# A hybrid attention layer: P's transposed blocks written to DRAM a pair later, and read back behind the next pair's first projection

## The chip, the core and the metric

The kernel runs on one core of a Trainium2 chip. TensorE (PE) multiplies, VectorE (DVE) and ScalarE (ACT) do elementwise work, GpSimd (POOL) and SyncE (SP) here mostly start transfers; transfers are also started from ScalarE's queue. The metric is device time in microseconds (us). The runs of the kernel before are 389.53, 388.30 and 389.66, with a median of 389.53.

## The reference

Input `x` is 512 rows of 1024 numbers, all float32. One layer:

```python
h = rms_norm(x, norm_w)
qa, ka, va, za, qb, kb, vb, zb, gl_a, gl_b = split(h @ w_in)   # eight parts of 512, two of 1024
qa, ka = rms_norm(heads(qa), q_norm_w), rms_norm(heads(ka), k_norm_w)     # 8 heads of 64
oa = moba_attention(qa, ka, va, rel_bias)         # softmax over causal scores plus a bias by distance
ob = stick_breaking_attention(qb, kb, vb)         # weights: sigmoid(z) times a product of (1 - sigmoid)
ya = (merge(oa) * silu(za)) @ w_up_moba
yb = (merge(ob) * silu(zb)) @ w_up_sb
y = sigmoid(gl_a + b_a) * ya + sigmoid(gl_b + b_b) * yb
out = x + y @ w_out
```

With 512 rows in two blocks of 256 and a top 3, the block selection of branch a takes every earlier block, so branch a is a plain causal softmax with a bias. Branch b is strictly causal.

## The kernel before, in words

Every large product is made in float32 accuracy out of three fast matmuls (lines 234 to 236): each operand is split into a high and a low part, ScalarE makes the high part of a weight tile (line 188, `wh<-wr`), VectorE the low part by subtraction (line 190, `wl<-wr,wh`). A weight tile `wr` of 512 KB is loaded by SP (lines 160 and 179). There are three buffers each for `wr`, `wh` and `wl`; a load waits until the low part of the tile three before it is made, and a split waits until TensorE is done with the tile three before.

The middle of the kernel, from 145.6 us on, is a loop over eight pairs of heads (`PAIRS`: pairs 0 to 3 are branch a, pairs 4 to 7 branch b). For a pair:

- TensorE makes the scores of both heads (line 513, `sa` or `sb`), in three groups of two PSUM banks, and then the weighted sum of values of the pair two before (line 608, `po<-pt,v`).
- VectorE and ScalarE turn the scores into weights P. In branch a: bias and row minimum (line 533), exponential (535), scaling (539, 541). In branch b: sigmoids on ScalarE (554, 555, 564, 565), then on VectorE scans (558, 568, `sx<-om`) and products (560, 570, `pb<-pb,sx`).
- P has to be transposed. VectorE transposes 32 by 32 blocks within each quarter of the partitions (line 580, `turned`, two buffers). The quarters are exchanged through DRAM: `put` writes the four quarters with four transfers of 160 KB on SP's queue (line 587, `pda`/`pdb`, four buffers), and `get` reads the whole back with one transfer of 640 KB on ScalarE's queue (line 594, `pta`/`ptb`, four buffers).
- Between these, projections are filled in as TensorE's work: three chunks of 24 matmuls a pair (`FILLS`: `gl` gates, `kb` keys, `zb` gates of branch b, `ya` the up-projection of branch a; pair 7 has more). `finish` multiplies the weighted sum by its gate (line 613, `oa`/`ob`) and splits it (761, 762).

PSUM has two banks named `pj` and six named `s`. A `pj` bank serves a projection or a weighted sum, so the second projection of a pair writes the bank that the weighted sum `po` leaves: it waits for line 613. The six `s` banks serve the scores and `ya`; the products with `ya` are taken out by line 780 (`gl<-ya,gl`).

Each engine executes its own instructions in order, and a queue starts its transfers in order. The order itself is fixed when the program is built, by a scheduler that takes instructions of all engines by data dependence and by its own estimate of when each could start; `tc.issue_after(i)` keeps an instruction behind `i` in that order. Each transfer that SP or ScalarE starts also takes one of eight completion counters in turn, and waits until that counter's last transfer has landed.

At the end of `b` = 1 of pairs 4, 5 and 6, `sum_w` makes sums of output weights by transfers of GpSimd; a copy of one number of `done[m, b]` holds them back until that read-back has landed (line 141).

Of the kernel before, what the change touches and what calls it, by code (L numbers as in the profile page):

```python
# [12 lines left out]
AF = mybir.ActivationFunctionType  # L13
# [28 lines left out]
SUMS = {(4, 1): ("T1a",), (5, 1): ("T1b",), (6, 1): ("T2a",)}  # L42
# [17 lines left out]
def hybrid_layer(ctx: ExitStack, tc: tile.TileContext, x, xT, w, rel, out):  # L60
    nc = tc.nc
    V, A, G, T = nc.vector, nc.scalar, nc.gpsimd, nc.tensor
# [13 lines left out]
    def bank(tag, name):  # L76
        return pp.tile([P, S], F32, tag=tag, bufs=BANKS[tag], name=name)

    def slot(name, dt=F32):
        return gp.tile([P, S], dt, tag="g", name=name)  # L80
# [32 lines left out]
    def wide(name):  # L113

        return vp.tile([P, H // 2, 2, P], F32, tag="v", name=name).rearrange("p a b d -> p (a b d)")
# [23 lines left out]
    def sum_w(names, done):  # L139

        with tc.issue_after(G.tensor_copy(turn_of, done[:1, :1].bitcast(F32)).ins):  # L141
            for n in range(2):
                for name in names:
                    if n == 0:
                        sums[name] = wide(name)
                    blk = TERMS[name[:2]][n]
                    src = sums[blk + name[2]] if blk[0] == "T" else w[WO + BLOCKS.index(blk + name[2])]
                    nc.gpsimd.dma_start(sums[name], src, **({"accum_op": ALU.add} if n else {}))
# [234 lines left out]
    def load_bias(h):  # L383
        bt = oms[h % 2][:, :S]
        nc.sync.dma_start(bt, bass.AP(tensor=e_dr.tensor, offset=e_dr.offset + h * TW, ap=[[1, P], [1, S]]))
        return bt
# [106 lines left out]
    def chunk_ct(name):  # L493
        hi, lo = load_w()
        ps = bank(home[0], name)
        for k in range(KT):
            ks = slice(k * P, (k + 1) * P)
            mm3(ps, hi[:, ks], lo[:, ks], xH[k], xL[k], k == 0, k == KT - 1)
        return ps


    def scores(br, p, q, k, res):

        (qh, ql), (kh, kl) = q[p], k[p]
        for grp in ((3,), (2,), (1, 0)):
            ps = [bank("s", f"s{br}{2 * p + b}{grp[0]}") for b in range(2)]
            c = 0
            for i in grp:
                n = (i + 1) * P
                for m, (x, y) in enumerate(((qh, kl), (ql, kh), (qh, kh))):  # L510
                    for b in range(2):
                        o = slice(b * HD, (b + 1) * HD)
                        T.matmul(ps[b][:, c:c + n], x[o, i * P:(i + 1) * P], y[o, :n], start=m == 0, stop=m == 2)  # L513
                for b in range(2):
                    res[2 * p + b][i] = ps[b][:, c:c + n]
                c += n
            for b in range(2):
                res[2 * p + b][grp] = ps[b][:, :c]
# [25 lines left out]
    evicted = []  # L544
# [31 lines left out]
    def turn(br, h, rows):  # L576
        turned = tp.tile([P, 4, 10, 32], F32, tag="turned", bufs=2, name=f"turned{br}{h}")
        for i, n in ((3, 4), (2, 3), ((1, 0), 3)):
            at = AT[i if i in (3, 2) else 1]
            V.transpose(turned[:, :, at:at + n, :].rearrange("p q j r -> p j q r"),  # L580
                        rows[i].rearrange("p (j q c) -> p j q c", j=n, q=4))
        return turned

    def put(br, h, turned):
        dr = dp.tile([P, 4 * PQ], F32, tag="pd", bufs=4, name=f"pd{br}{h}")
        for a in range(4):
            nc.sync.dma_start(bass.AP(tensor=dr.tensor, offset=dr.offset + a * PQ,
                                      ap=[[4 * PQ, 32], [32 * 4 * PQ, 4], [1, PQ]]),
                              turned[a * 32:(a + 1) * 32].rearrange("c q k r -> c q (k r)"))
        return dr  # L590

    def get(br, h, dr):
        pt = tp.tile([P, 4 * PQ], F32, tag="pt", bufs=4, name=f"pt{br}{h}")
        nc.scalar.dma_start(pt, dr)
        return pt

    ocol = {}
# [17 lines left out]

    zr, qb, kb = {}, [], []

    def f_z(br, p):
        ps = chunk_ct(f"z{br}{p}")
        zr[br, p] = slot(f"z{br}{p}")  # L620
        A.activation(zr[br, p], ps, AF.Sigmoid)
        V.tensor_tensor(zr[br, p], ps, zr[br, p], op=ALU.mult)

    def f_q(p):
# [7 lines left out]
    def f_g(i):  # L632
        ps = chunk_ct(f"gl{i}")
        g = slot(f"gl{i}")
        evicted.append(A.activation(g, ps, AF.Identity if raw[0] else AF.Sigmoid, bias=mb[:, i:i + 1]).ins)  # L635
        gates[i] = g

    raw = [False]

    def f_s(i):  # L640
        with tc.issue_after(evicted[-1]):
# [2 lines left out]
    for i, word in enumerate(FRONT):  # L644
        kind, n = word.split(":")
        f_g(int(n)) if kind == "g" else f_z("a", int(n))
        if i == 0:
            norm(ps_ka, "ka", after=summed[0])
            mix_x(0)
        elif i == 1:  # L650
            mix_x(1)
            summed.append(each(add_sum, "v", ("T3",), last["ka"]))
        elif i == 2:
            bring("qa")
            mix_x(2)
        elif i == 3:
            spread(ps_ka, "ka")
            mix_x(3)
        elif i == 4:
            bring("ka")  # L660
        elif i == 5:
            qa.extend(split_flipped(raws["qa"], "qa"))
# [152 lines left out]
    def split_3(k):  # L815
# [3 lines left out]


    make = {"za": lambda i: f_z("a", i), "zb": lambda i: f_z("b", i), "q": f_q, "k": f_k, "g": f_g, "s": f_s,
            "up": lambda i: up("a", i)}
    fills = [[(kind, int(i)) for kind, i in (word.split(":") for word in part.split())] for part in FILLS]

    def fill(tag="pj"):

        for kind, i in fills.pop(0):
            home[0] = "s" if kind == "up" else tag
            make[kind](i)

    PAIRS = [("a", p) for p in range(H // 2)] + [("b", p) for p in range(H // 2)]
    done = {}

    def head(m, b):
        return PAIRS[m][0], 2 * PAIRS[m][1] + b

    def finish(m, tag="s"):

        br, p = PAIRS[m]
        weighted(tag, br, p, v_of[br], [done.pop((m, b)) for b in range(2)])  # L840
        split_o(br, p)

    early[0] = True
    for m, (br, p) in enumerate(PAIRS):
        raw[0] = br == "a"
        q, k = (qa, ka) if br == "a" else (qb, kb)
        sc = {h: {} for h in (2 * p, 2 * p + 1)}
        with tc.issue_after(end[0]):
            scores(br, p, q, k, sc)
        if m > 1:  # L850
            finish(m - 2, "pj")
        for b in range(2):
            h = 2 * p + b
            bias = load_bias(h) if br == "a" else None
            done[m, b] = put(br, h, turn(br, h, (softmax if br == "a" else stick)(h, sc[h], bias)))
            fill()
            if not b:
                done[m, 0] = get(*head(m, 0), done[m, 0])
        for b in range(2):
            if not b:  # L860
                done[m, 1] = get(*head(m, 1), done[m, 1])
            if (m, b) in SUMS:
                sum_w(SUMS[m, b], done[m, b])
            fill("pj" if (b or not fills[1]) and m < 7 else "s")
    fill()
    for m in (6, 7):
# [160 lines left out]
```

## Time and profile before

| | |
|---|---|
| runs, us | 389.53, 388.30, 389.66 |
| the profiled execution: time, span | 388.29, 386.5 |
| granted TensorE clock | 1.000 |
| TensorE busy | 379.2 us (98%), 1935 matmuls |
| VectorE, ScalarE, GpSimd busy | 284.5, 211.2, 80.0 us |
| loads `wr<-in_w` on SP | 57 of 512 KB, 5.5 us from issue to landing (median) |
| writes `pda`, `pdb` on SP | 32 and 32 of 160 KB, 2.9 and 3.2 us |
| read-backs `pta`, `ptb` on ScalarE's queue | 8 and 8 of 640 KB, 5.1 and 4.9 us |

The time of an execution is 1.8 us more than its span from first to last instruction. Matmuls overlap, so TensorE's busy time is not its floor; the distance between starts of matmuls (0.23 us for 512 columns) shows where it stands still. A row of a timeline has start, duration, engine, line, operation, tiles written and read, partitions and elements, the count, and in square brackets how long the engine had been idle and what ended that. SPq and ACTq are queues that start transfers.

### The profile page before, as it was taken

The numbers are of one execution on the slowest core, as the hardware profiler recorded it, in microseconds if no ns is written. First come the engines' busy times: TensorE is split into PE (matmuls) and PEld (weight loads), VectorE is DVE, ScalarE is ACT, GpSimd is POOL, SyncE is SP. The second block draws the span as 40 slices with busy tenths as digits, with TensorE's granted clock in tenths as the row PEclk, the third lists the DMA queues.
The fourth block names the chain that finished last, engine by engine and source line by source line (L and its number), as shares of the span: only waits on it lengthen the run. The fifth ranks groups of instructions, "written<-read, shape, count | busy, mean of one in ns | idle before, by whom it ended". The sixth has DMA issues, their size and how long they took to land.

```text
span 386.5 us, 5481 instructions
## 1 busy us (share of the span) xinstructions
PE 379.2 (98%) x1935; PEld 308.3 (80%) x1935; DVE 284.5 (74%) x487; ACT 211.2 (55%) x367; POOL 80.0 (21%) x124
## 2 busy tenths in 40 slices
PE   8999999999999999999999999999999999999996
PEld 4888888888888998887878877776777877888885
DVE  4828999945777468972965399599939926999963
ACT  5685567338764447782853494554628213368540
POOL 3859959120210200000000000020101000420310
PEclk9999999999999999999999999999999999999999
DMA  7989799986864745569846826977697784599965
GB/s 264 342 332 336 198 234 274 283 277 238 209 173 100 190 124 187 146 204 335 242 110 207 308 69 213 303 181 226 190 332 257 159 331 132 173 254 294 177 155 175
DMA packets 36747, 86.38 MB, mean 223 GB/s; under 512 B 3944, under 2 KB 16744, under 8 KB 36720
## 3 DMA queue, kind: packets, MB, share of 16 engines
q1 hardware_dynamic: 27696, 52.72, 41.6%
q0 software_dynamic: 6576, 22.57, 24.6%
q10 hardware_dynamic: 2448, 10.75, 8.1%
q8 instruction: 15, 0.25, 0.2%
q14 instruction: 12, 0.10, 0.1%
HBM read 67.65 MB, written 14.70 MB: 213 GB/s over the span
## 4 chain that ended last, share of the span: by engine, by line
PE 82%; DVE 6%; DMA 5%; ACT 3%; issue 2%; SPq 2%; DVEq 0%
PE gl L234 6%; PE gl L235 6%; PE gl L236 6%; DMA pdb<-turnedb 3%; PE sa L513 2%; DMA wr<-in_w 2%; PE yb L234 2%; PE yb L235 2%; PE ka L235 2%; PE ka L234 2%; PE vx L235 2%; PE vx L234 2%; PE za L235 2%; PE za L234 2%; PE ka L236 2%; PE yb L236 2%
## 5 line engine op out<-in xcount | busy, mean ns | idle before, releaser
L190 DVE TENSOR_TENSOR wl<-wr,wh 128x1024 fp32r<-128x1024 f32 (+1 forms) x61 | 71.6, 1178 | 24.5 <-ACT wh L188 24.1
L188 ACT ACTIVATE wh<-wr 128x1024 fp32r<-128x1024 f32 (+1 forms) x61 | 63.2, 1036 | 46.2 <-DMA wr<-in_w 25.1
L234 PE MATMUL gl<-xl,wh 128*128 128x512 f32 x128 | 50.0, 391 | 0.0
L235 PE MATMUL gl<-xh,wl 128*128 128x512 f32 x128 | 49.8, 389 | 0.0
L236 PE MATMUL gl<-xh,wh 128*128 128x512 f32 x128 | 49.8, 389 | 0.0
L141 POOL COPY turn_of<-ptb 1x1 f32<-1x1 f32 x3 | 2.3, 758 | 148.9 <-DMA ptb<-pdb 148.9
L234 PEld LDWEIGHTS gl<-xl,wh 128*128 128x128 f32 x128 | 24.0, 188 | 5.2 <-issue 0.2
L236 PEld LDWEIGHTS gl<-xh,wh 128*128 128x128 f32 x128 | 24.0, 188 | 5.0
L235 PEld LDWEIGHTS gl<-xh,wl 128*128 128x128 f32 x128 | 24.0, 188 | 4.9
L635 ACT ACTIVATE gl<-gl,x 128x512 f32<-128x512 f32 x16 | 11.0, 685 | 20.8 <-PE gl L236 20.0
L533 DVE CUSTOM_DVE_ANT_0 pa<-sa,om 128x512 f32<-128x512 f32 (+3 forms) x32 | 13.9, 483 | 9.5 <-DMA om<-e_dr 6.8
L535 ACT ACTIVATE pa<-pa,m 128x512 f32<-128x512 f32 (+3 forms) x32 | 17.6, 552 | 5.0 <-DVE m L533 5.0
L558 DVE TENSOR_TENSOR_SCAN sx<-om,begin 128x512 f32<-128x512 f32 (+1 forms) x16 | 16.6, 1073 | 0.0
L580 DVE STREAM_TRANSPOSE turneda<-pa 128x384 f32<-128x384 f32 (+1 forms) x24 | 13.8, 605 | 2.6 <-ACT pa L539 2.4
L235 PE MATMUL ya<-oha,wl 128*128 128x512 f32 x32 | 12.8, 401 | 1.8 <-DVE wl L190 1.8
L580 DVE STREAM_TRANSPOSE turnedb<-pb 128x384 f32<-128x384 f32 (+1 forms) x24 | 13.6, 594 | 0.0
L234 PE MATMUL zb<-xl,wh 128*128 128x512 f32 x32 | 12.9, 404 | 0.0
L234 PE MATMUL kb<-xl,wh 128*128 128x512 f32 x32 | 12.7, 398 | 0.0
L234 PE MATMUL yb<-olb,wh 128*128 128x512 f32 x32 | 12.6, 393 | 0.0
L235 PE MATMUL zb<-xh,wl 128*128 128x512 f32 x32 | 12.5, 391 | 0.0
L236 PE MATMUL ya<-oha,wh 128*128 128x512 f32 x32 | 12.5, 390 | 0.0
L235 PE MATMUL yb<-ohb,wl 128*128 128x512 f32 x32 | 12.5, 390 | 0.0
(430 smaller groups left out, 1066.1 us busy)
## 6 DMA issues: line engine op xcount, KB each, us to landing
wr<-in_w SPq DMA_DIRECT2D x57, 512.0 KB, 5.5
pda<-turneda SPq DMA_DIRECT2D x32, 160.0 KB, 2.9
pta<-pda ACTq DMA_DIRECT2D x8, 640.0 KB, 5.1
pdb<-turnedb SPq DMA_DIRECT2D x32, 160.0 KB, 3.2
ptb<-pdb ACTq DMA_DIRECT2D x8, 640.0 KB, 4.9
qT<-in_w POOLq DMA_DIRECT2D x6, 512.0 KB, 5.9
xn<-in_x SPq DMA_DIRECT2D x8, 256.0 KB, 5.9
om<-e_dr SPq DMA_DIRECT2D x8, 256.0 KB, 4.3
```

Source lines behind the costliest of these rows:

```text
L141: with tc.issue_after(G.tensor_copy(turn_of, done[:1, :1].bitcast(F32)).ins):
L188: high[c] = A.activation(hi[:, a:b], raw[:, a:b], AF.Copy).ins
L190: low[c] = V.tensor_tensor(lo[:, a:b], raw[:, a:b], hi[:, a:b].bitcast(F32), op=ALU.subtract).ins
L234: T.matmul(ps, aH, bL, start=start, stop=False, skip_group_check=on)
L235: T.matmul(ps, aL, bH, start=False, stop=False, skip_group_check=on)
L236: end[0] = T.matmul(ps, aH, bH, start=False, stop=stop, skip_group_check=on).ins
L513: T.matmul(ps[b][:, c:c + n], x[o, i * P:(i + 1) * P], y[o, :n], start=m == 0, stop=m == 2)
L533: V.tensor_tensor_reduce(rows[i], sc[i], bias[:, S - n:], scale=1.0, scalar=3e38, op0=ALU.add, op1=ALU.min, accum_out=m[:, 0, i:i + 1])
L535: A.activation(rows[i], rows[i], AF.Exp, bias=m[:, 0, i:i + 1], scale=-1.0, accum_out=m[:, 1, i:i + 1])
L558: V.tensor_tensor_scan(sx[:, n - 1::-1] if n == S else sx[:, :n][:, ::-1], om[:, S + 1 - n:][:, ::-1], begin[:, S - n:S][:, ::-1], 0.0, op ...
L580: V.transpose(turned[:, :, at:at + n, :].rearrange("p q j r -> p j q r"), rows[i].rearrange("p (j q c) -> p j q c", j=n, q=4))
L635: evicted.append(A.activation(g, ps, AF.Identity if raw[0] else AF.Sigmoid, bias=mb[:, i:i + 1]).ins)
```

## The change

The pair's two `put`s are no longer recorded right behind the transposes, but after the next pair's scores; its two `get`s are recorded behind the first projection (or other fill) of the next pair, and `tc.issue_after(mark[0])` keeps them behind that projection's eviction on ScalarE (`zr` or `gl`; a pair whose first fill is a key projection has the gate before it as its mark). Pair 7, which has no next pair, does both as before. The three `sum_w` calls hang on the read-back of the pair before, at the same places of the loop. No operation is added or removed; no buffer count changes.

```diff
     def get(br, h, dr):
         pt = tp.tile([P, 4 * PQ], F32, tag="pt", bufs=4, name=f"pt{br}{h}")
-        nc.scalar.dma_start(pt, dr)
+        with tc.issue_after(mark[0]):
+            nc.scalar.dma_start(pt, dr)
         return pt
...
+    raw, mark = [False], [None]
+
     def f_z(br, p):
         ps = chunk_ct(f"z{br}{p}")
         zr[br, p] = slot(f"z{br}{p}")
-        A.activation(zr[br, p], ps, AF.Sigmoid)
+        mark[0] = A.activation(zr[br, p], ps, AF.Sigmoid).ins
...
         evicted.append(A.activation(g, ps, AF.Identity if raw[0] else AF.Sigmoid, bias=mb[:, i:i + 1]).ins)
+        mark[0] = evicted[-1]
...
-    done = {}
+    done, turned = {}, {}
...
         with tc.issue_after(end[0]):
             scores(br, p, q, k, sc)
+        for b in range(2) if m else ():
+            done[m - 1, b] = put(*head(m - 1, b), turned.pop(b))
         if m > 1:
             finish(m - 2, "pj")
         for b in range(2):
             h = 2 * p + b
             bias = load_bias(h) if br == "a" else None
-            done[m, b] = put(br, h, turn(br, h, (softmax if br == "a" else stick)(h, sc[h], bias)))
+            turned[b] = turn(br, h, (softmax if br == "a" else stick)(h, sc[h], bias))
+            if m == 7:
+                done[m, b] = put(br, h, turned.pop(b))
             fill()
-            if not b:
+            for n in range(2) if m and not b else ():
+                done[m - 1, n] = get(*head(m - 1, n), done[m - 1, n])
+            if m == 7 and not b:
                 done[m, 0] = get(*head(m, 0), done[m, 0])
         for b in range(2):
-            if not b:
+            if m == 7 and not b:
                 done[m, 1] = get(*head(m, 1), done[m, 1])
             if (m, b) in SUMS:
-                sum_w(SUMS[m, b], done[m, b])
+                sum_w(SUMS[m, b], done[m - 1, b])
             fill("pj" if (b or not fills[1]) and m < 7 else "s")
```

The scheduler makes a new order of this on every engine but for most of TensorE's. Three places follow. (Line numbers behind 600 are larger by 1, later by 3, in the changed kernel: 594 is 595, 613 is 614, 780 is 783.)

SP's queue, from pair 3's weights to pair 6's. Before, with `pda` or `pdb` the writes of one head, `wr` a load of a weight tile:

```order
L160 DMA wr_2341<-in_w 128x1024
L587 DMA pda_2190<-turneda_2186 32x4x320 x4
L587 DMA pdb_2332<-turnedb_2328 32x4x320 x4
L587 DMA pdb_2395<-turnedb_2391 32x4x320 x4
L160 DMA wr_2404<-in_w 128x1024
L160 DMA wr_2439<-in_w 128x1024
L160 DMA wr_2558<-in_w 128x1024
L160 DMA wr_2621<-in_w 128x1024
L587 DMA pdb_2549<-turnedb_2545 32x4x320 x4
L587 DMA pdb_2612<-turnedb_2608 32x4x320 x4
L160 DMA wr_2656<-in_w 128x1024
```

The changed kernel, from the same place on:

```order
L587 DMA pda_2284<-turneda_2179 32x4x320 x4
L160 DMA wr_2332<-in_w 128x1024
L160 DMA wr_2392<-in_w 128x1024
L160 DMA wr_2425<-in_w 128x1024
L587 DMA pdb_2496<-turnedb_2324 32x4x320 x4
L587 DMA pdb_2501<-turnedb_2384 32x4x320 x4
L160 DMA wr_2549<-in_w 128x1024
L160 DMA wr_2609<-in_w 128x1024
L160 DMA wr_2642<-in_w 128x1024
L587 DMA pdb_2709<-turnedb_2541 32x4x320 x4
L587 DMA pdb_2714<-turnedb_2601 32x4x320 x4
```

The tiles `wr_2404` and `wr_2439` (the second projection and `ya` of pair 5) stood behind both of pair 4's writes; now `wr_2392` and `wr_2425`, the same weights, stand ahead of them.

VectorE at the end of pair 6, from its last transposes to pair 7's first scan. Before, with `wl_2768` the low part of the tile that pair 6's `ya` multiplies with:

```order
L580 STREAM_TRANSPOSE turnedb_2821<-pb_2803 128x3x4x32
L190 TENSOR_TENSOR wl_2768<-wr_2656,wh_2767 128x1024
L622 TENSOR_TENSOR zb_2798<-zb_2773,zb_2798 128x512
L780 TENSOR_TENSOR gl_746<-ya_2871,gl_746 128x512
L780 TENSOR_TENSOR gl_1646<-ya_2872,gl_1646 128x512
L190 TENSOR_TENSOR wl_2831<-wr_2771,wh_2830 128x1024
L613 TENSOR_TENSOR ob_2947<-pob_2936,zb_2585 128x512
L190 TENSOR_TENSOR wl_2866<-wr_2834,wh_2865 128x1024
L762 TENSOR_TENSOR olb_2950<-ob_2947,ohb_2949 128x512
L558 SCALAR_TENSOR_TENSOR sx_2958<-om_121,begin 128x512
```

The changed kernel, from pair 7's first tile of the up-projection to the same `ob`:

```order
L190 TENSOR_TENSOR wl_2977<-wr_2855,wh_2976 128x1024
L558 SCALAR_TENSOR_TENSOR sx_2954<-om_121,begin 128x512
L558 SCALAR_TENSOR_TENSOR sx_2959<-om_120,begin 128x384
L560 TENSOR_TENSOR pb_2950<-pb_2950,sx_2954 128x512
L560 TENSOR_TENSOR pb_2951<-pb_2951,sx_2959 128x384
L580 STREAM_TRANSPOSE turnedb_2967<-pb_2950 128x4x4x32
L568 SCALAR_TENSOR_TENSOR sx_2964<-om_short,begin 128x386
L580 STREAM_TRANSPOSE turnedb_2967<-pb_2951 128x3x4x32
L570 TENSOR_TENSOR pb_2949<-pb_2949,sx_2964 128x384
L558 SCALAR_TENSOR_TENSOR sx_3021<-om_121,begin 128x512
L614 TENSOR_TENSOR ob_2943<-pob_2932,zb_2576 128x512
```

`wl` splits moved forward by a pair's scans, and `ob`, which stood ahead of pair 7's first scan, now stands behind three scans of pair 7's first head and one of its second. In the changed kernel the low part for pair 6's `ya` stands ahead of pair 6's first scan:

```order
L190 TENSOR_TENSOR wl_2606<-wr_2549,wh_2605 128x1024
L190 TENSOR_TENSOR wl_2639<-wr_2609,wh_2638 128x1024
L783 TENSOR_TENSOR gl_637<-ya_2644,gl_637 128x512
L783 TENSOR_TENSOR gl_701<-ya_2645,gl_701 128x512
L190 TENSOR_TENSOR wl_2759<-wr_2642,wh_2758 128x1024
L558 SCALAR_TENSOR_TENSOR sx_2741<-om_121,begin 128x512
```

There `wl_2759` answers to `wl_2768` of before.

More of the change, by code (lines that the diff above doesn't have):

```diff
@@ L635, in f_g @@
         evicted.append(A.activation(g, ps, AF.Identity if raw[0] else AF.Sigmoid, bias=mb[:, i:i + 1]).ins)
+        mark[0] = evicted[-1]
         gates[i] = g
-    raw = [False]
     def f_s(i):
```

## The prediction

> **What bounds the kernel now.** I read the page first, then TensorE's timeline, the stretches by pair, and at last the queues and engines around the places where TensorE stands still.
>
> ```profile
> PE 379.2 (98%) x1935; PEld 308.3 (80%) x1935; DVE 284.5 (74%) x487; ACT 211.2 (55%) x367; POOL 80.0 (21%) x124
> PE 82%; DVE 6%; DMA 5%; ACT 3%; issue 2%; SPq 2%; DVEq 0%
> ```
>
> TensorE is the bound: 98% busy, 82% of the chain that ended last. A change of transfers can only give back time in which TensorE stands still, and lose time by making it stand still. So the question is where it does. These are its starts at the head of each section in pairs 4 to 7:
>
> ```profile
> 234.59 0.44 PE L234 MATMUL kb<-xl,wh 128*128 128x512 f32 x1
> 240.19 0.50 PE L513 MATMUL sb<-kb1l,qb1h 64*128 64x512 f32 x2
> 244.57 0.50 PE L234 MATMUL zb<-xl,wh 128*128 128x512 f32 x1
> 250.14 0.39 PE L234 MATMUL gl<-xl,wh 128*128 128x512 f32 x1
> 255.58 0.61 PE L234 MATMUL ya<-ola,wh 128*128 128x512 f32 x2
> 256.70 0.50 PE L235 MATMUL ya<-oha,wl 128*128 128x512 f32 x1 [0.51 <-DVE wl L190]
> 261.91 0.50 PE L513 MATMUL sb<-kb2l,qb2h 64*128 64x512 f32 x2
> 264.05 0.38 PE L513 MATMUL sb<-kb2l,qb2h 64*128 64x256 f32 x1 [0.64 <-ACT pb L555]
> 267.96 0.50 PE L234 MATMUL zb<-xl,wh 128*128 128x512 f32 x1
> 278.98 0.39 PE L234 MATMUL ya<-ola,wh 128*128 128x512 f32 x1
> 280.71 0.50 PE L235 MATMUL ya<-oha,wl 128*128 128x512 f32 x1 [1.34 <-DVE wl L190]
> 286.19 0.50 PE L513 MATMUL sb<-kb3l,qb3h 64*128 64x512 f32 x2
> ```
>
> An undisturbed chunk of 24 matmuls ahead of scores takes 240.19 - 234.59 = 5.60. The first `ya` chunk took 261.91 - 255.58 = 6.33, so it lost 0.73; the second 286.19 - 278.98 = 7.21, so it lost 1.61. Scores and weighted sum took 244.57 - 240.19 = 4.38 in pair 5, but 267.96 - 261.91 = 6.05 in pair 6: 1.67 lost, more than the 0.64 in brackets, since the two heads, which otherwise run side by side on the halves of the array, were pulled apart. Together 4.01. The stretches by pair say the same:
>
> ```profile
> core 0: us, PE busy (x) PEld busy (x) DVE busy (x) ACT busy (x) POOL busy (x), PEclk, DMA share, GB/s
> 219.20:240.19 20.99, 20.99 (x117) 16.50 (x116) 18.40 (x31) 15.95 (x32) 0.00 (x0) 1.00 0.49 148
> 240.19:261.91 21.72, 21.21 (x117) 16.49 (x116) 17.46 (x25) 11.36 (x20) 2.06 (x3) 1.00 0.82 239
> 261.91:286.19 24.28, 22.30 (x118) 17.09 (x118) 20.04 (x30) 12.73 (x24) 2.23 (x3) 1.00 0.78 239
> ```
>
> Pairs 5 and 6 are 0.73 and 3.29 longer than pair 4, at a clock of 1.00 throughout. Elsewhere from 145 us to the end of the matmuls I find no gap over 0.15 us, so 4.0 is all that there is to win.
>
> Why was TensorE late there? SP's queue:
>
> ```profile
> 154.70 20.00 SPq L587 DMA_DIRECT2D pda<-turneda  x16
> 174.80 0.95 SPq L160 DMA_DIRECT2D wr<-in_w  x2
> 232.80 10.14 SPq L587 DMA_DIRECT2D pdb<-turnedb  x8
> 243.04 6.96 SPq L160 DMA_DIRECT2D wr<-in_w  x4
> 255.57 9.52 SPq L587 DMA_DIRECT2D pdb<-turnedb  x8
> 265.18 0.92 SPq L160 DMA_DIRECT2D wr<-in_w  x1
> SPq L587 <- DVE turnedb L580: 44.5, 8, 8.6
> ```
>
> The writes stand in the queue and wait for VectorE's transposes, 44.5 us in all in branch b alone, and loads of weights stand behind them. In pair 5 the load issued at 243.04 stood behind both writes of pair 4. What came of it on the engines:
>
> ```profile
> 216.61 0.69 DVE L533 CUSTOM_DVE_ANT_0 pa<-sa,om 128x512 f32<-128x512 f32 x1 [6.26 <-DMA om<-e_dr]
> 247.32 1.06 ACT L188 ACTIVATE wh<-wr 128x1024 fp32r<-128x1024 f32 x1 [1.28 <-DMA wr<-in_w]
> 248.29 0.58 ACT L554 ACTIVATE om<-sb 128x512 f32<-128x512 f32 x1
> 249.56 2.06 DVE L558 TENSOR_TENSOR_SCAN sx<-om,begin 128x512 f32<-128x512 f32 x2
> 279.47 1.18 DVE L190 TENSOR_TENSOR wl<-wr,wh 128x1024 fp32r<-128x1024 f32 x1
> ```
>
> Pair 5's scores began at 240.19, but ScalarE took up their sigmoids at 248.29, since a split that waited for the load stood ahead; VectorE's scans began at 249.56. From there VectorE never caught up (20.04 busy in pair 6's 24.28), and the split for pair 6's `ya`, last in its order, began at 279.47: the stall at 280.71. In pair 3 a bias tile, too, was 6.26 late behind writes.
>
> **The change part by part.** Nothing is added; 64 writes and 16 read-backs keep size and queue, so no instruction is to be paid for. What moves is order.
>
> *The writes.* Nothing in the data holds a write until the scores: it waits for its transposes, and SP reaches it sooner than these are done. So the writes start about when they did. What changes is what stands behind them: three tiles ahead of both writes of a pair, not up to two tiles ahead and two behind. I walked the changed order with the durations above. The load at 174.80 becomes possible at about 162, behind the split that frees its buffer; pair 3's bias is asked for when pair 2's is read (about 187), so the 6.26 goes; pair 5's tiles can be asked for at about 214, 216 and 222 (each when the split of the tile three before is done), where two of them went out from 243.04 on. With them ScalarE comes to pair 5's sigmoids 1.8 us behind the start of the scores (key split 0.6, weight split 1.06) and not 8.1 behind. In pair 6 ScalarE and VectorE begin with pair 6's own `ya` tile, so the split is made some 13 us ahead of its use (two chunks, the scores and the weighted sum come first: 5.6 + 5.4 + 4.4, less the 2.4 that it takes). Both `ya` stalls go: 0.73 + 1.61.
>
> *The scores of pair 6.* Before, their third group was put into the bank of the pair's own first group, and waited for ScalarE to read it (264.05). In the changed order it takes the banks of `ya`, as pair 7's did before:
>
> ```profile
> 286.30 0.69 DVE L780 TENSOR_TENSOR gl<-ya,gl 128x512 f32<-128x512 f32 x1 [2.03 <-PE ya L236]
> ```
>
> That is done 0.8 behind the start of pair 7's scores at 286.19; the third group starts 1.3 behind, and pair 7 lost nothing. In pair 6 VectorE has to be free at that moment: I get it free 1.5 us earlier. So 1.67 goes too. Cover gone, it costs what VectorE is late beyond 0.5 us.
>
> *The weighted sums.* The second projection of a pair writes the bank that `po` leaves, so it waits for line 613. That product now stands behind four scans in pair 7, and similarly in pairs 4 to 6. Durations:
>
> ```profile
> 251.55 1.13 DVE L560 TENSOR_TENSOR pb<-pb,sx 128x512 f32<-128x512 f32 x2
> 252.60 0.95 DVE L568 TENSOR_TENSOR_SCAN sx<-om_short,begin 128x386 f32<-128x386 f32 x1
> 253.47 0.69 DVE L580 STREAM_TRANSPOSE turnedb<-pb 128x512 f32<-128x512 f32 x1
> 254.08 0.51 DVE L570 TENSOR_TENSOR pb<-pb,sx 128x384 f32<-128x384 f32 x1
> 290.68 0.69 DVE L613 TENSOR_TENSOR ob<-pob,zb 128x512 f32<-128x512 f32 x1 [2.56 <-PE pob L608]
> ```
>
> Starts follow each other 0.07 closer than the durations. Pair 7 from the start of its scores: high part 0.2 to 1.3, low part to 2.4, two scans 2.0, two products 1.05, transpose 0.6, scan 0.9, transpose 0.5, product 0.45, scan 1.1, and `ob` from 9.0 to 9.7. The projection wants the bank at 250.14 - 240.19 = 9.95. That leaves 0.25; the same sum leaves 0.7 in pair 4, 0.7 in pair 5 (keys and queries split in between) and 1.4 in pair 6. VectorE's work in pair 6, 20.04, is under the 20.99 of an undisturbed pair, so lateness doesn't pile up. I take 0.3 us lost in all, which is VectorE 0.55 later than walked (0.3 in pair 7); bounds: nothing, and 0.75 if it is 0.8 later in all four pairs.
>
> *The read-backs.* They go 10.5 us or so later than they could, two at once, behind the eviction of the first projection:
>
> ```profile
> DMA to landing us min/median/max: 3.8/5.0/7.9
> DMA to landing us min/median/max: 2.1/3.8/7.9
> ```
>
> The first row is of the read-backs, the second of branch b's writes with read-backs. In pair 5 they start at about 240.19 + 10.8 = 251.0 and are needed behind pair 6's scores, which begin at 261.1 without the 0.73, so at 263.2: 12.2 us, against 5.0 for one and 10.0 if one followed the other. Nothing lost; 3.6 a pair if both took 7.9 one behind the other. The last pair's reads go about when ScalarE reaches them, 12 us ahead of their use.
>
> On ScalarE's queue the waits ahead of the read-backs were short before:
>
> ```profile
> L594 ACTq EVENT_SEMAPHORE  x32: 17/38/38, 160.8 to 312.9; - x32
> ```
>
> They stay short if the writes are down when ScalarE comes to the read-back. Pair 4's second write is issued by about 241, and with the longest 7.9 it lands at 249, ahead of 251; in pair 3 the margin is some 4 us. I cost it at nothing. The Trainium skill, page DMA: Bandwidth & Descriptors, section Anatomy of one DMA, says that a transfer's wait for a semaphore is held by the sequencer that issues it, before dispatch, and not by the DMA engines; SP's 44.5 us are of that kind. By that rule a write that lands later than its read-back's turn stops ScalarE's splits and sigmoids too, which speaks against reads on this queue; the sum by it is the same up to 10 us of landing, and beyond that it is worse by each us, which is in the third rival's chance.
>
> *The sums on GpSimd* hang on read-backs some 10 to 20 us earlier. They feed the output stage, which did not wait for them; bounds nothing and 0.2.
>
> **Sum.** 0.73 + 1.61 + 1.67 - 0.3 = 3.7. The profiled execution took 388.29, so 384.6. The median of the runs, 389.53, stands 1.24 above that execution; on it the forecast is **385.8**, with its own range from 384.6 to 387.2.
>
> **Rivals.**
>
> *VectorE, not the loads, makes `ya` late.* For: 18.40, 17.46 and 20.04 of work in three pairs of 21, and the chain behind 249.56 runs through scans. Then pair 4 gives its delay on, both `ya` stalls stay, and only the bank of pair 6's scores, 1.67, is won: 387.9. Against: 8.1 us between scores and sigmoids in pair 5 were a load's, and the split for `ya` now stands ahead of the scans. 0.18.
>
> *Slower: the weighted sums hold up the projections.* If VectorE comes to line 613 by d later than walked in each of pairs 4 to 7, TensorE loses (d - 0.7) twice, d - 1.4 and d - 0.25. At d = 1.75 that is 4.0, and the gain is gone; at d = 2.6 it is 7.4, and the time 389.53 + 3.4 = 392.9. For: the margins are small, one scan more ahead of it is 1.1, and VectorE has no slack in a pair beyond 1 to 3 us. Against: all durations in the walk are this execution's own, and the pairs before 4 lost nothing. 0.14.
>
> *Slower: the read-backs are late.* Two landings in series at the longest, 15.8 against 12.2, cost 3.6 in each of six pairs: 21.6 - 4.0 above before, 407.1. It decides from 12.2 us on. The same slow transfers would stop ScalarE at read-backs whose write is not down. Against: the median of 5.0, and that the writes and loads around them are the same bytes as before. 0.03.
>
> **How the numbers follow.** Forecast 0.60, VectorE 0.18, weighted sums 0.14, read-backs 0.03, a mixture of small gains and losses 0.05. The runs of before spread by 0.35%, so I take 0.5%, 1.95 us, as what can be told from no change. Faster: 0.60 and a part of the second, 0.65. Same: the rest of the second and the mixture, 0.20. Slower: 0.15. The range from 384.0, nothing given back and a run like the lowest, to 388.9, the second case (387.9) and 1.0 above it, leaves out about 0.2.
>
> **What would show it.** Right: no idle time ahead of `ya` for a low part; pair 6's scores and weighted sum in 4.4 us; pairs 4 to 7 each 20.9 to 21.3 long; SP issuing pair 5's three tiles before 225; ScalarE's `om` in pair 5 about 242. The small loss would be TensorE's first matmul of `gl` waiting for line 614 in pair 7. Wrong, and the forecast with it: TensorE waiting at that place in each pair, or at `po` for a read-back, or VectorE's split for `ya` still ending a wait.

## The result: 385.8 us, with a new stall in pair 4

Five runs of the changed kernel gave 385.51 to 386.76, with a median of **385.8 us**; five of the kernel before beside them gave 388.30 to 389.66, with a median of 389.12. The ratio is 0.9921 (95% interval 0.9899 to 0.9942), so the change makes the kernel faster by about 0.8%. The profiled execution took 385.65, with a span of 383.8 where before had 386.5: 2.7 less.

The page of the changed kernel, the row of the engines and the first row of the chain that ended last:

```profile
PE 378.3 (99%) x1935; PEld 308.7 (80%) x1935; DVE 285.1 (74%) x487; ACT 212.0 (55%) x367; POOL 77.9 (20%) x124
PE 95%; DVE 3%; ACT 1%; issue 0%; DVEq 0%
```

The engines' work is what it was (VectorE 284.5 before, ScalarE 211.2); TensorE's share of the chain is 95% and was 82%. What has gone is time in which TensorE stood still. Its timeline at the places the prediction spoke of, and the one row of the loop that has a wait:

```profile
236.19 0.50 PE L234 MATMUL kb<-xl,wh 128*128 128x512 f32 x1 [1.12 <-DVE zb L625]
257.29 0.39 PE L234 MATMUL ya<-ola,wh 128*128 128x512 f32 x1
262.82 0.50 PE L513 MATMUL sb<-kb2l,qb2h 64*128 64x512 f32 x2
264.89 2.38 PE L609 MATMUL pob<-ptb,vbs 128*64 128x128 f32 x20
278.21 0.39 PE L234 MATMUL ya<-ola,wh 128*128 128x512 f32 x1
283.74 0.50 PE L513 MATMUL sb<-kb3l,qb3h 64*128 64x512 f32 x2
```

Both `ya` chunks take 262.82 - 257.29 = 283.74 - 278.21 = 5.53, where they took 6.33 and 7.21. Pair 6's scores take 2.07 to the start of the weighted sum, where they took 3.74. One wait is new: the first matmul of `kb3` in pair 4 waits for line 625, the product that finishes the gate `zb0`. By pairs:

```profile
219.53:241.90 22.37, 21.25 (x117) 16.49 (x117) 17.23 (x24) 13.13 (x22) 0.74 (x2) 1.00 0.56 176
241.90:262.82 20.92, 20.92 (x117) 16.57 (x117) 18.93 (x27) 10.64 (x19) 1.69 (x3) 1.00 0.80 240
262.82:283.74 20.92, 20.92 (x117) 16.58 (x117) 18.48 (x26) 13.67 (x25) 1.74 (x3) 1.00 0.87 258
```

Pairs 5 and 6 are now 20.92, with TensorE busy all through. Pair 4 grew from 20.99 to 22.37: 1.38 given back.

SP's queue shows what made the difference (its timeline from pair 4 on, and its wait for branch b's transposes):

```profile
215.83 7.06 SPq L160 DMA_DIRECT2D wr<-in_w  x3
230.04 2.78 SPq L587 DMA_DIRECT2D pdb<-turnedb  x4
237.11 1.93 SPq L587 DMA_DIRECT2D pdb<-turnedb  x4
...
251.94 8.94 SPq L587 DMA_DIRECT2D pdb<-turnedb  x8
260.98 4.62 SPq L160 DMA_DIRECT2D wr<-in_w  x3
...
SPq L587 <- DVE turnedb L580: 44.8, 8, 7.2
```

Pair 5's three tiles go out from 215.83 to 222.89; before, two of them went out from 243.04. Pair 4's writes start at 230.04, and at 232.80 before. SP waits for the transposes just as long as before, 44.8 against 44.5, but no load that is needed soon stands behind it.

### The profile page after: what moved, and what is told of

It reads as the page before. It is cut to its first block, busy times and chain, and to the rows that moved or that the text cites. A ratio compares the mean times of both kernels' runs of the same rounds, so it can differ in the third digit from the quotient of the medians.

```text
span 383.8 us, 5482 instructions
## 1 busy us (share of the span) xinstructions
PE 378.3 (99%) x1935; PEld 308.7 (80%) x1935; DVE 285.1 (74%) x487; ACT 212.0 (55%) x367; POOL 77.9 (20%) x124
## 4 chain that ended last, share of the span: by engine, by line
PE 95%; DVE 3%; ACT 1%; issue 0%; DVEq 0%
PE gl L234 7%; PE gl L236 7%; PE gl L235 7%; PE pob L609 2%; PE sa L513 2%; PE kb L234 2%; PE yb L234 2%; PE yb L235 2%; PE kb L235 2%; PE ka L234 2%; PE kb L236 2%; PE ya L235 2%; PE ya L234 2%; PE vx L236 2%; PE za L236 2%; PE za L234 2%
## 5 line engine op out<-in xcount | busy, mean ns | idle before, releaser
L235 PE MATMUL kb<-xh,wl 128*128 128x512 f32 x32 | 12.5, 391 | 0.0
L235 PE MATMUL ka<-wh,xl 128*128 128x512 f32 x32 | 12.5, 390 | 0.0
```

The source lines that it names most:

```text
L235: T.matmul(ps, aL, bH, start=False, stop=False, skip_group_check=on)
```

## Experiments

The kernels below were timed beside the kernel before: swapped fills, late writes only, late reads only and writes on GpSimd beside 23 runs of it with a median of 388.57, the other four beside 11 with a median of 388.72. The column "pairs 4 to 7" is the stretch from pair 4's first score matmul to the weighted sum behind pair 7, read off TensorE's timeline of each profiled execution; 94.56 recurs in all kernels in which TensorE doesn't wait there. Each kernel was scheduled anew when it was built, so the orders of the engines differ among them by more than the lines shown. The stretches of late reads only and of writes on GpSimd come from executions that took 387.41 and 388.47, at a granted clock of 1.000; the medians of these two kernels are above what their traces show.

| kernel | median, us | ratio to before (95%) | pairs 4 to 7, us | TensorE's waits there |
|---|---|---|---|---|
| before | 389.12 | 1 | 99.01 | `wl` twice, bank of the scores |
| changed | 385.80 | 0.9921 (0.9899 to 0.9942) | 96.01 | `kb3` for `zb0` |
| swapped fills | 384.35 | 0.9889 (0.9871 to 0.9907) | 94.56 | none |
| late writes only | 384.27 | 0.9887 (0.9869 to 0.9905) | 94.56 | none |
| late reads only | 389.06 | 1.0021 (1.0001 to 1.0040) | 98.31 | scores twice, `wl` |
| writes on GpSimd | 389.96 | 1.0040 (1.0017 to 1.0063) | 98.74 | `kb3` for `zb0`, `gl` for `ob` |
| writes on GpSimd, late reads, swapped fills | 384.18 | 0.9884 (0.9865 to 0.9903) | 94.56 | none |
| all late but pair 4 | 384.30 | 0.9883 (0.9867 to 0.9899) | 94.56 | none |
| only pair 4 late | 394.19 | 1.0131 (1.0102 to 1.0160) | 105.80 | `gl` for `oa`, `wl` twice, bank of the scores |
| reads behind the 2nd fill | 396.87 | 1.0206 (1.0187 to 1.0225) | 105.97 | `pob` for read-backs |

### Which half of the change brings the gain?

Late writes only (against the changed kernel):

```diff
         for b in range(2) if m else ():
             done[m - 1, b] = put(*head(m - 1, b), turned.pop(b))
+        for n in range(2) if m else ():
+            done[m - 1, n] = get(*head(m - 1, n), done[m - 1, n])
...
             fill()
-            for n in range(2) if m and not b else ():
-                done[m - 1, n] = get(*head(m - 1, n), done[m - 1, n])
```

> The changed kernel with one half of the change undone: the writes are recorded behind the next pair's scores, the read-backs right behind those writes and not behind the first fill. The loads on SP stand ahead of the writes as in the changed kernel. Queue theory (loads behind waiting writes made both ya chunks and pair 6's third score group late): the three stalls of the kernel before, 0.73, 1.61 and 1.67 us, are gone, the time is within 1 us of the changed kernel's, 385 to 387. Rival, that the gain came from the read-backs' later place on ScalarE's queue (ScalarE no longer held at them): the ya stalls come back, 388 to 389.5.

Late reads only (against the changed kernel):

```diff
-        for b in range(2) if m else ():
-            done[m - 1, b] = put(*head(m - 1, b), turned.pop(b))
...
-            turned[b] = turn(br, h, (softmax if br == "a" else stick)(h, sc[h], bias))
-            if m == 7:
-                done[m, b] = put(br, h, turned.pop(b))
+            done[m, b] = put(br, h, turn(br, h, (softmax if br == "a" else stick)(h, sc[h], bias)))
```

> The other half alone: the read-backs behind the next pair's first fill, the writes recorded where the kernel before has them, right behind the transposes. On SP loads stand behind waiting writes as in the kernel before. Queue theory: the ya chunks of pairs 5 and 6 still wait for the low part of their weights, the sections of pairs 5 and 6 stay longer than 21 us, and the time is near the kernel before, 388 to 390. Rival, that the read-backs' place brought the gain: 385 to 387 and no wait for the low part.

Measured: 384.27 and 389.06. The late writes, with the read-backs right behind them, bring all of the gain, and more than the whole change does; the late read-backs alone bring none in the median, and 0.7 us in the stretch of the profiled execution (98.31 for 99.01). With late reads only, SP has writes and loads interleaved as before, and TensorE's timeline shows the old stalls in a new mixture:

```profile
263.25 0.38 PE L513 MATMUL sb<-kb2l,qb2h 64*128 64x256 f32 x1 [0.64 <-ACT pb L555]
265.19 0.39 PE L513 MATMUL sb<-kb2l,qb2h 64*128 64x256 f32 x1 [1.44 <-DVE gl L783]
306.67 0.50 PE L235 MATMUL ya<-oha,wl 128*128 128x512 f32 x1 [0.35 <-DVE wl L190]
```

The time came out as expected, but not the places: pair 6's `ya` took 5.53 and waited for nothing, pair 5's took 5.78, and most of the loss, 2.84 us, lay in pair 6's scores, 4.91 to the weighted sum where 2.07 is undisturbed. ScalarE came to pair 5's sigmoids at 247.22 there, 7.3 behind the scores at 239.94; before it was 8.1, and in the changed kernel 1.55:

```profile
243.45 0.59 ACT L554 ACTIVATE om<-sb 128x512 f32<-128x512 f32 x1
```

### Are the loads the cause, or VectorE?

The kernel before, with only the queue of the writes changed:

```diff
-            nc.sync.dma_start(bass.AP(tensor=dr.tensor, offset=dr.offset + a * PQ,
+            nc.gpsimd.dma_start(bass.AP(tensor=dr.tensor, offset=dr.offset + a * PQ,
```

> The kernel before with only the writes of P's quarters started from GpSimd's queue and not from SP's; everything is recorded where the kernel before has it, so no load of weights can stand behind a write. Queue theory: pair 5's and 6's tiles go out as soon as a buffer is free, the three stalls go and the time falls to between 385 and 387, near the changed kernel's. Rival, that VectorE and not the loads made ya late: both ya stalls stay (2.3 us together), 387.5 to 389.5. What GpSimd takes to start a transfer is not in the rows of the kernel before for this form; if it is much longer than SP's, the read-backs come later, against 12 us of room.

Measured: 389.96, above even the rival's range, and not for the rival's reason. Of the old stalls none is left; the `ya` chunks take 5.54 and 5.53, and pair 6's scores 2.07. Two others came, in all of TensorE's waits from the loop to the end:

```profile
235.78 0.50 PE L234 MATMUL kb<-xl,wh 128*128 128x512 f32 x1 [1.12 <-DVE zb L622]
295.91 0.47 PE L234 MATMUL gl<-xl,wh 128*128 128x512 f32 x1 [2.46 <-DVE ob L613]
```

So both theories failed in their numbers: the queue theory was right on the three stalls and blind to what replaced them. The first of the two is the changed kernel's. The second is the place of the second rival, the `pj` bank that `po` leaves in pair 7, and its chain runs back to a read-back (GpSimd's, ScalarE's and VectorE's timelines):

```profile
279.13 0.91 POOL L148 DMA_DIRECT2D T1b<-in_w  x1 [3.50 <-DMA T1b<-in_w]
284.58 0.56 POOL L587 DMA_DIRECT2D pdb<-turnedb  x1 [1.75 <-issue]
287.30 0.33 ACTq L594 DMA_DIRECT2D ptb<-pdb  x1
287.67 0.60 ACT L554 ACTIVATE om<-sb 128x512 f32<-128x512 f32 x1 [6.47 <-DMA pdb<-turnedb]
295.08 0.68 DVE L613 TENSOR_TENSOR ob<-pob,zb 128x512 f32<-128x512 f32 x1
```

The last of pair 6's writes went out at 284.58; its read-back stood on ScalarE's queue until 287.30, ahead of pair 7's sigmoids, and ScalarE was idle for 6.47 us. The transposes of pair 6 had ended at 279.00, those of its first head at 273.05; but on GpSimd's queue a load for a sum (`T1b`), held until 279.13 by the transfer before it, stood ahead of six of the eight writes. The trap of SP's queue had moved to GpSimd's. The rule of the Trainium skill that the prediction cites (DMA: Bandwidth & Descriptors, Anatomy of one DMA: the issuing sequencer holds the wait) agrees with ScalarE's row: the price was ScalarE's, and through `ob` TensorE's 2.6 us.

To see whether this read-back and the wait at `kb3` are what ate the gain, the last kernel of this group has the writes on GpSimd, the read-backs behind the first fill as in the changed kernel, and the two fills of pair 4 swapped (next section):

> Writes recorded as in the kernel before but started from GpSimd's queue, read-backs as in the changed kernel behind the first fill, the two fills of pair 4 swapped. With the writes on GpSimd alone TensorE lost 2.6 us at the second projection of pair 7, behind ScalarE's sigmoids, which stood 6.47 us behind a read-back that waited for its write, and 1.3 us at kb3. Theory (a read-back in front of a write that is not down stops ScalarE's own work; later read-backs don't): both waits go, 384 to 385.5. Rival, that the writes' issue from GpSimd, interrupted by the loads of T1 and T2, is itself too slow: the read-backs wait still, ScalarE is held behind pair 5's or 6's first fill, and the time stays at 387 or more.

Measured: 384.18, and no wait in the stretch. That VectorE makes `ya` late is thereby refuted twice: with all writes where VectorE makes them, and its work unchanged (77.64 us in the stretch, against 78.46 before), no `ya` waits. And the late read-backs do have a use, one that the kernel with late writes on SP doesn't need. ScalarE still stands behind writes that are not down, 2.66 us until 254.68 and 3.47 us until 301.84, so the theory's "later read-backs don't" was too strong; but it now stands ahead of weight splits and not of a pair's sigmoids, and TensorE loses nothing by it.

### What is the new stall in pair 4?

Two fills of the changed kernel in the other order:

```diff
-         "zb:0", "g:11", "k:3 q:3 s:3 s:4", "",
+         "g:11", "zb:0", "k:3 q:3 s:3 s:4", "",
```

> The changed kernel with the first two fills of pair 4 in the other order: the gate projection gl11 comes first, zb0 second. In the changed kernel TensorE loses 1.3 to 1.4 us in pair 4, where the key projection kb3 wants the pj bank of zb0 and the product that empties it (line 625) stands behind scans in VectorE's order. Bank theory: kb3 then takes the bank that ScalarE empties for gl11, the stall goes, pair 4 falls from 22.4 to about 21.0 us, the time is 1.3 to 1.4 below the changed kernel's, about 384.4 (ratio to the kernel before 0.988 to 0.989). Rival, that VectorE is simply 1.4 us late in pair 4 and TensorE has to wait for it somewhere: the stall moves to another matmul of pair 4 or 5 and the time stays at about 385.8.

Measured: 384.35, with pair 4 at 20.92, so the bank theory holds to 0.1 us. VectorE's timeline in pair 4 shows how the change made the stall. Before:

```profile
233.80 0.68 DVE L622 TENSOR_TENSOR zb<-zb,zb 128x512 f32<-128x512 f32 x1
234.40 2.06 DVE L558 TENSOR_TENSOR_SCAN sx<-om,begin 128x512 f32<-128x512 f32 x2
```

The product ended at 234.48 and `kb3` began at 234.59. In the changed kernel:

```profile
230.51 2.06 DVE L558 TENSOR_TENSOR_SCAN sx<-om,begin 128x512 f32<-128x512 f32 x2
...
233.54 0.96 DVE L568 TENSOR_TENSOR_SCAN sx<-om_short,begin 128x386 f32<-128x386 f32 x1
...
235.02 0.52 DVE L570 TENSOR_TENSOR pb<-pb,sx 128x384 f32<-128x384 f32 x1
235.46 0.68 DVE L625 TENSOR_TENSOR zb<-zb,zb 128x512 f32<-128x512 f32 x1
```

VectorE reaches the second head's scans 3.9 us earlier (230.51 against 234.40), since pair 3's softmax no longer runs into pair 4; and the scheduler now puts the `zb0` product behind seven instructions of that head (three scans, three products, a transpose), where it stood ahead of all of them. It ends at 236.14, 1.2 after `kb3` could have begun (229.48 + 5.44 = 234.92). Earlier scans went ahead of a product that TensorE waits for. In the kernel with late writes only, the product stands before the short scan, at 233.38, and nothing waits.

### Does a pair's lateness come from its own loads?

Only pair 4 late: writes and read-backs of pair 4 are recorded behind pair 5's scores, those of all other pairs right behind the transposes (`LATE = (4,)` in the guards of both); the complement has `LATE = (0, 1, 2, 3, 5, 6)`.

```diff
+    LATE = (4,)
...
-        for b in range(2) if m else ():
+        for b in range(2) if m - 1 in LATE else ():
             done[m - 1, b] = put(*head(m - 1, b), turned.pop(b))
+        for b in range(2) if m - 1 in LATE else ():
+            done[m - 1, b] = get(*head(m - 1, b), done[m - 1, b])
```

> Only pair 4's writes and read-backs are recorded late, behind pair 5's scores; all other pairs as in the kernel before. On SP's queue pair 5's three tiles then stand ahead of both of pair 4's writes, but in pair 6 the tiles of the second projection and of ya stand behind both of pair 5's writes, as pair 5's did before. Queue theory (what is late in a pair comes from the loads behind the writes of the pair before, and the delay is handed on by VectorE): pair 5's ya loses nothing (0.73 gained), pair 6 now has pair 5's old delay, so a first ya wait of 0.5 to 1 us stays there, the scores of pair 6 and the 1.34 of its ya go or shrink: 385 to 387. Rival, that each stall has its own cause in its own pair: only 0.73 is gained, about 388, with 1.67 and 1.61 in place.

> The complement: every pair but pair 4 (and pair 7) has its writes and read-backs late; pair 4's are recorded where the kernel before has them. The scheduler, however, puts pair 5's three tiles ahead of pair 4's writes on SP all the same, since its neighbours' writes stand elsewhere. Queue theory (only the place on SP's queue counts, not the place where a write is recorded): none of the three stalls, 384 to 386. Rival, that pair 4's read-backs and writes in their old place hold ScalarE and VectorE: the stalls of pairs 5 and 6 stay, 387.5 to 389.5.

Measured: 394.19 and 384.30. The complement is as the queue theory has it: pair 4's writes are recorded where they were, but SP has pair 5's tiles at 219.42, ahead of the writes at 230.90, and all three stalls are gone. Where a write is recorded doesn't count; which loads stand behind it on the queue does.

With only pair 4 late, the theory was right on where and far off on how much. Pair 5's `ya` loses nothing (5.53); the delay moved to pair 6, as expected. ScalarE's and TensorE's timelines:

```profile
269.87 1.06 ACT L188 ACTIVATE wh<-wr 128x1024 fp32r<-128x1024 f32 x1 [3.77 <-DMA wr<-in_w]
271.35 0.58 ACT L554 ACTIVATE om<-sb 128x512 f32<-128x512 f32 x1
279.84 0.50 PE L235 MATMUL ya<-oha,wl 128*128 128x512 f32 x1 [1.85 <-DVE wl L190]
289.19 1.17 PE L513 MATMUL sb<-kb3l,qb3h 64*128 64x256 f32 x2 [2.41 <-DVE gl L783]
319.74 0.50 PE L235 MATMUL gl<-xh,wl 128*128 128x512 f32 x1 [1.69 <-DVE wl L190]
```

Pair 6's sigmoids start at 271.35, 9.45 behind its scores at 261.90, again behind a split that waits for a load. What pair 5 paid with 0.73 and handed on as 3.28, pair 6 paid with 2.15 in its `ya`, 3.90 in pair 7's scores, 2.15 in the weighted sum behind them and 2.00 in a later `gl`: 105.80 - 94.56 = 11.2 with small change, against 4.45 before. The 3.90 and the 2.15 behind it are one stop of 2.41 us and, for most of the rest, matmuls at half clock (last section). The 385 to 387 that I expected took the old delay's price for its price anywhere.

### What is the room for the read-backs?

The swapped-fills kernel with the read-backs behind the second fill:

```diff
-            for n in range(2) if m and not b else ():
+            for n in range(2) if m and b else ():
                 done[m - 1, n] = get(*head(m - 1, n), done[m - 1, n])
```

> The changed kernel with the two fills of pair 4 swapped, and the read-backs one fill later, behind the eviction of the second fill. ScalarE's order then has pair 4's read-backs behind the eviction of gl in pair 5, which it makes only after pair 6's first sigmoids: in the kernel with swapped fills at 264.4, where the weighted sum pob starts at 263.75. Read-backs landed there in 4.8, 6.5 and at most 8.6 us. Window theory (a read-back costs nothing until it lands behind its weighted sum, then each us one us): pair 4's read-backs go out at 265 to 266, land at 271 to 274, and TensorE loses 7 to 10 us at the weighted sum of pair 6; at the other pairs the window is about 6.8 and the loss 0 to 1 us each. 392 to 397, with TensorE waiting at pob for a transfer. Rival, that TensorE finds the lost time again later, or that the landing is much faster when both go alone: under 390.

Measured: 396.87, at the upper end of the range. The read-backs of pair 4 on ScalarE's queue, and who waits for them:

```profile
266.01 0.33 ACTq L595 DMA_DIRECT2D ptb<-pdb  x1
266.45 0.37 ACTq L595 DMA_DIRECT2D ptb<-pdb  x1
271.13 0.69 PE L609 MATMUL pob<-ptb,vbs 128*64 128x128 f32 x2 [5.03 <-DMA ptb<-pdb]
274.12 4.53 PE L609 MATMUL pob<-ptb,vbs 128*64 128x128 f32 x18 [2.30 <-DMA ptb<-pdb]
```

They are 5.1 and about 7.6 us under way, and TensorE waits for each. Pair 6's scores and weighted sum take 14.6 where 4.4 is undisturbed, pairs 3 and 4 lose 0.6 and 0.7. The place from which the read-backs cost something lies between the first fill's eviction, which is free, and the second's.

## Why the prediction was right, and where only its sum was

The forecast was 385.8 and the median is 385.8, but two errors cancel in it. By its own steps:

**The three stalls (0.73 + 1.61 + 1.67): right.** All are gone, for the reason given; late writes only, the complement of pair 4 and the writes on GpSimd show the loads behind waiting writes as the cause. The walk's times hold: pair 5's tiles out at 215.83 to 222.89 (forecast 214 to 222), ScalarE at pair 5's sigmoids 1.55 behind the scores (1.8), and in pair 6 the low part for `ya` ready 13 us ahead of use:

```profile
262.93 0.69 DVE L783 TENSOR_TENSOR gl<-ya,gl 128x512 f32<-128x512 f32 x1 [1.10 <-PE ya L236]
264.02 1.23 DVE L190 TENSOR_TENSOR wl<-wr,wh 128x1024 fp32r<-128x1024 f32 x1 [0.40 <-ACT wh L188]
```

The first row also frees the bank for pair 6's third score group 0.8 behind the scores' start, as the prediction took from pair 7. What was to be won was a little more than I added up: the gaps under 0.15 us that I left out, 0.07 of them in the chunk of 5.60 that I took for undisturbed, make 99.01 - 94.56 = 4.45 of 4.01. The 1.67 went by a new order on VectorE, as forecast. All eight kernels in which pair 5's tiles go out early have that order, and the two others (before and late reads only) don't; no run has early loads with the old order, so for this stall the two are not told apart.

**The weighted sums (0.3 given back): the step that failed, in its size and place.** Line 614, where I looked, lost nothing:

```profile
228.42 0.65 DVE L614 TENSOR_TENSOR oa<-poa,za 128x512 f32<-128x512 f32 x1
250.29 0.68 DVE L614 TENSOR_TENSOR oa<-poa,za 128x512 f32<-128x512 f32 x1
270.79 0.68 DVE L614 TENSOR_TENSOR ob<-pob,zb 128x512 f32<-128x512 f32 x1
292.62 0.67 DVE L614 TENSOR_TENSOR ob<-pob,zb 128x512 f32<-128x512 f32 x1
293.69 0.39 PE L234 MATMUL gl<-xl,wh 128*128 128x512 f32 x1
```

With the bank wanted 9.95 behind each pair's scores, it was free 0.4, 0.9, 1.3 and 0.4 us ahead (pairs 4 to 7); the forecast had 0.7, 0.7, 1.4 and 0.25. But the same mechanism, a product behind scans that keeps a `pj` bank, struck at the other bank: pair 4 is the one pair of branch b whose third fill is a projection into a `pj` bank and not `ya`, and it takes the bank of the first fill, `zb0`. That cost 1.38 and was not in the walk, which followed one bank of the two. Swapping two fills took it away. So the sign that I gave, pairs 4 to 7 each 20.9 to 21.3 long, held for pairs 5 and 6 (20.92) and not for pair 4 (22.37); pair 7 has more fills and takes 31.80 to its weighted sum even undisturbed.

**The read-backs (nothing): right.** They went out at 252.76 and were needed at 264.89, 12.1 us later (forecast 12.2), with these times to landing, so there were 5 us to spare:

```profile
DMA to landing us min/median/max: 4.5/6.2/6.9
```

Once the margin is gone, though, the third rival's price of 1 us per us is too low (last section).

**The sums on GpSimd (nothing): right as far as seen.** The stretch behind the loop, from pair 7's weighted sum to the end, is 68.3 us before and after; they were not moved by themselves.

**From the profiled execution to the median (+1.24): wrong.** I carried the distance of before's median over to a kernel without its stalls. The profiled execution took 385.65, 1.05 above the 384.6 of the sum, and the median stood only 0.15 above that. Before's larger samples have medians of 388.57 and 388.72, so its profiled run was 0.3 to 0.4 from the middle and not 1.24. The stretch of pairs 4 to 7 gained 3.00 (4.45 less 1.45); the start of pair 4, which lies between 219.02 and 219.84 in the executions in which nothing waits before it, took 0.33 of it.

**The rivals.** VectorE as the cause is refuted. The weighted sums' mechanism is real, but in the changed kernel it cost 1.38 of the 4.0 that the rival needs to eat the gain, and at another place; at the place that the rival names it came with the writes on GpSimd (2.6 us in pair 7) and with only pair 4 late (0.5 us in pair 5). The read-backs became late only when moved by another fill.

## What to carry to other kernels

On an in-order queue, a transfer that waits for work costs what stands behind it: put loads that could go now ahead of writes that can't, and read the queue's order, not the place in the source. When a stall is taken away, walk every buffer that the freed engine's earlier work can now get in front of (here both PSUM banks, not one). A stall's price belongs to its place: the same kind of delay cost 4.4 us in one pair and 11.2 in the next, so half of a reordering can be worse than none. A new order can bring a stall of its own: look at all of TensorE's waits again, not at the old ones alone.

## What the runs showed of the hardware

**A stop of TensorE can cost a slower clock afterwards.** In the profiled executions of the two slowest kernels the granted clock fell; in those of all others it stayed at 1.00 in the stretch. With the read-backs behind the second fill (columns as in the stretches above):

```profile
263.97:271.13 7.16, 2.13 (x25) 1.85 (x24) 6.65 (x9) 7.06 (x15) 0.00 (x0) 0.87 0.96 346
271.13:278.58 7.45, 5.14 (x20) 3.25 (x20) 2.39 (x4) 1.19 (x3) 0.73 (x2) 0.50 0.63 172
```

After 5 us of standing still the clock was 0.50 for the whole weighted sum. Of the 10.7 us lost here (14.6 - 4.4, and 0.45 in the next chunk), 7.3 are waits, and the other 3.3 or so go with the matmuls at the lower clock. With only pair 4 late, the weighted sum after the stop of 2.41 ran at 0.50 too; with the writes on GpSimd a stop of 2.46 left the clock at 1.00:

```profile
291.25:295.71 4.46, 4.46 (x21) 2.14 (x20) 4.30 (x7) 3.46 (x8) 0.00 (x0) 0.50 0.41 148
...
295.91:297.50 1.59, 1.59 (x7) 1.34 (x8) 1.59 (x3) 1.59 (x3) 0.88 (x2) 1.00 0.84 270
```

The Trainium skill, TensorE: Matmul & The Clock Gate, section Part 1: The HAM clock gate, says that the clock is full or half by the activity in a window of about 3.4 us that runs freely. Half speed after a stop, and two stops of one length with different outcomes, agree with that; that 2.41 us sufficed once is less than the whole idle window that it names. The times of executions beyond the traced one fit this: of the twelve of late reads only, two had a clock of 1.000 and took 387.14 and 387.41, and the ten at 0.990 to 0.996 took 388.85 to 391.99. That short stops are what slowed these ten is likely, and not shown.

**The same writes made fewer packets on GpSimd's queue.** Rows of the queues, of the kernel before and of that with the writes on GpSimd:

```profile
q1 hardware_dynamic: 27696, 52.72, 41.6%
q0 software_dynamic: 6576, 22.57, 24.6%
```

```profile
q0 software_dynamic: 9648, 33.06, 33.4%
q1 hardware_dynamic: 18480, 42.23, 32.0%
```

The 64 writes, 10.49 MB, were 9216 packets on SP's queue (8192 of 1280 bytes and 1024 of 4 bytes, by the traces) and 3072 on GpSimd's (2048 of 5120 bytes and 1024 of 4 bytes). The median from issue to landing of branch b's writes was 5.8 us on GpSimd's queue and 3.2 before; why, these runs don't tell.
